# Five ordered places, a later set of splits, and four more convolution taps off VectorE in a two-layer trunk

## The chip, the cores and the metric

The kernel runs on one core of a Trainium2 chip. The core has five engines that run their own instruction lists and meet through semaphores: TensorE (PE in the profile; its weight loads are listed apart, as PEld), VectorE (DVE), ScalarE (ACT), GpSimd (POOL) and SyncE (SP), which here issues nearly all transfers. Matmuls write to PSUM, a memory of few 128x512 banks; the other operands lie in SBUF. The metric is the time of one execution on the device in microseconds, the median of several executions.

## What is computed

The input x has 1024 tokens of 1024 channels in float32. Layer 0 feeds one projection to two branches, layer 1 is a convolution module:

```python
# layer 0
u, gate_s, q, k, v, gate_r = split(rmsnorm(x) @ w_ab)
y  = gelu(s5(u))                                  # diagonal complex state space, chunks of 64 tokens
ys = y * sigmoid(y @ glu_w + glu_b) * silu(gate_s)
yr = headnorm(retention(rope(q), rope(k), v)) * silu(gate_r)
x1 = x + concat(ys, yr) @ w_out
# layer 1
a, b, g = split(rmsnorm(x1) @ w_c)
c  = causal_depthwise_conv(a * sigmoid(b), width=31) + bias
z  = silu(layernorm_channels(c)) * silu(g)
x2 = x1 + z @ w_out_c
out = rmsnorm(x2)
```

The matmuls keep float32 accuracy: each operand is split into a high part rounded to the matmul's format (h) and the rest (l), and each product is three matmuls, wh x xh, wh x xl and wl x xh (L224 to L226).

## The kernel before, in words

Channels lie on the 128 partitions, in eight blocks of 128; tokens run along the free dimension in two halves of 512, so nearly every tile is 128x512. Names carry the block and the half: `cv6_1` is block 6 of half 1. The trace leaves these numbers out; the lists of instructions shown below keep a half or block and a running number of the tile.

A weight block is loaded by SP as `wf` (128x1024), rounded on ACT to `wh`, and `wl = wf - wh` is made on POOL, for some matrices on DVE (L214). Weights that both halves use are stored as `lo` and loaded again in half 1 (L181, L199). Buffers of one tag go round in a ring: a load waits on SP until the last reader of the buffer it takes is done, and what SP has behind it waits too. The tag `tp` has three buffers. It serves, one after the other, the loads `yr0f`, the first five taps of each convolution block, and the gate loads `gl` of blocks 0 to 2 of half 1.

The program is written stage by stage, and a scheduler orders each engine's list by the position in the program, by priorities (`self.at`) and by a model of durations. `self.order` adds pairs: on that engine's list, the first instruction (name of the output and how manyth write of it) comes after the second. A pair sets an order on one engine only. `issue_after` does the same for one instruction or a group of them.

The places that are touched:

- *The end of the state space and retention* (350 to 530 us). POOL makes the rotary product `qswp` (L1153) and the rest `wl` of the weights for v (L214). DVE makes `yn`, the input of the gelu (L1039 to L1042), and `kraw` (L1138), a projection taken from PSUM. SP stores blocks of gated sums (`t_d`, L1049) and loads `gs`, from which sums of gating weights are made, and `yp`, the next part of y; the gelu of `yp` (L1031) stands on ACT ahead of copies of v from PSUM (L1188), for whose bank PE waits (L1185).
- *The gated unit* (530 to 620 us), in `layer0_back_and_layer1`. PE forms block products `mm_glu`. DVE combines them with earlier sums into `mm_gluy` (half 0, L1453) and `mm_gluz` (half 1, L1470), which takes a product from its PSUM bank and so lets PE use the bank again. `gated` (L1396) then passes each through a tanh on ACT, a product with the gate `yg` made on POOL (L1401), and two instructions on DVE (L1414, L1418). `load_split` (L1346) loads the eight retention blocks `yr0f` and splits them: `yr0h` on ACT, `yr0l` on DVE (L1334). The output projection `mm_wo` multiplies `ys`, then `yr`.
- *The convolution* (640 to 1066 us). `conv` (L1566) does two blocks at a time. ACT makes taps 0 to 4, POOL adds them, and ACT copies the sum into a PSUM accumulator `cv`. DVE adds the other 26 taps, one `scalar_tensor_tensor` each (L1607): shifted u times the tap's weight, plus `cv`. From block 4 on, the `pilot`, a mean over the first four blocks, is taken off ahead of the last tap (L1596), which writes `co`. Block 7 of half 1 is the last; its last tap is in `conv_norm_wide` and goes into the channel sum `cs` as well (L1687 to L1689). `cq` is the sum of squares (L1693). PE sums both over the channels (`cst`, L557), and from them come the mean and the scale of the normalisation. Ahead of these two sums PE has matmuls of the last projection's half 0 (`mm_oc`), and behind them 66 more. The additions `x` (L1769) take `mm_oc` from PSUM and add `x1l`, loaded by SP.

Of the kernel before, what the change touches and what calls it, by code (L numbers as in the profile page):

```python
# [11 lines left out]
F32 = mybir.dt.float32  # L12
# [3 lines left out]
ALU = mybir.AluOpType  # L16
# [3 lines left out]
P = 128  # L20
# [13 lines left out]
LO_V = {f"g{i}" for i in range(1, 10)} | {"u4", "u5", "u6", "wos", "wor"}  # L34
NORM_TAP = 23, 11
G0 = 3


LANES = 2


def s5_order():
# [28 lines left out]
def un(ap):  # L71

    return ap.rearrange("p (c a) -> p a c", a=LANES)


def nat(ap):

    return ap.rearrange("p (a c) -> p a c", a=LANES)

# [15 lines left out]
class Trunk:  # L95
# [148 lines left out]
    def run(self):  # L244
        tc, nc, A = self.tc, self.nc, self.A
        self.ps_mm = self.pool("ps_mm", 3, PSUM)
        self.cp = self.pool("cp")
        self.wp = self.pool("wp")
        self.opA = self.pool("opA", 16)
        self.dram = self.pool("dram", 1, DRAM)  # L250

        self.ident = self.cp.tile([P, P], F32, name="ident")
        make_identity(nc, self.ident)
        self.ones = self.cp.tile([P, P], F32, name="ones")
        nc.vector.memset(self.ones[:], 1.0)
        self.ones_r = self.cp.tile([P, P], F32R, name="ones_r")
        nc.vector.tensor_copy(self.ones_r[:], self.ones[:])
        self.epst = self.cp.tile([P, 1], F32, name="epst")
        nc.vector.memset(self.epst[:], EPS)
        self.mhalf = self.cp.tile([P, KB], F32, name="mhalf")  # L260
        nc.vector.memset(self.mhalf[:], -0.5)
        self.warm = self.cp.tile([P, 1], F32, name="warm")
        nc.scalar.copy(self.warm[:], self.ones[:, 0:1])

        dt = lambda n, shape: self.dram.tile(shape, F32, name=n)
        self.u_d = dt("u_d", [8, 8, 16, 8, P])
        self.y_d = dt("y_d", [8, 8, 16, 8, P])
        self.k_d = dt("k_d", [8, 112 + P, P])
        self.gs_d = dt("gs_d", [D, T])
        self.gr_d = dt("gr_d", [D, T])  # L270
        self.yn_d = dt("yn_d", [D, T])
        self.yr_d = dt("yr_d", [D, T])
        self.t_d = dt("t_d", [2, 2, HALF, T])
        self.x1_d = dt("x1_d", [D, T])

        with ExitStack() as mid:
            self.mid = self.pool("mid", 1, stack=mid)
            with ExitStack() as st:
                self.layer0_front(st)
            with ExitStack() as st:  # L280
                self.ps_aux = self.pool("ps_aux", 5, PSUM, stack=st)
                self.retention(st)
        with ExitStack() as st:
            self.layer0_back_and_layer1(st)
        self.order(s5_order())

    def order(self, pairs):

# [1047 lines left out]
    def layer0_back_and_layer1(self, st):  # L1336
# [54 lines left out]
        def spare(name, n):  # L1391
            return ps_cv.tile([P, HALF], F32, name=name, tag=("cv", "cn")[n % 2])

        held = []

        def gated(nb, h, z, turned=False):  # L1396
            yg = lp.tile([P, HALF], F32, name=f"yg{nb}_{h}", tag="u", bufs=5)
# [63 lines left out]
        for m in range(2):  # L1461
            pss = [self.bank(f"mm_glu5{2 * m + a}", aux=False) for a in range(2)]
            for i, x in ((5, t1), (3, b22)):
                w = wn()
                for a in range(2):
                    n = 2 * m + a
                    product(pss[a], w, a, x, i == 3)
                    if i == 5:
                        z = spare(f"mm_gluz{n}", n)
                        v.tensor_tensor(nat(z[:]), un(u3[n][:]), un(pss[a][:]), op=ALU.add)  # L1470
                        gated(4 + n, 1, z, True)
                    else:
                        v.tensor_tensor(pss[a][:], u2[n][:], pss[a][:], op=ALU.add)
                        glu_end = gated(n, 1, pss[a])
        yr = [load_split([self.yr_d[rows(k), hs(h)] for k in range(KB)], f"yr{h}", h, False) for h in range(2)]


        hx = [None, None]
# [87 lines left out]
        def conv(h, n2):  # L1566
# [4 lines left out]
            for nb in (n2, n2 + 1):  # L1571
# [14 lines left out]
                        nc.scalar.copy(acc[:], s0[:])  # L1586
                accs_.append(acc)
                outs.append(opB.tile([P, HALF], F32, name=f"co{nb}_{h}", tag="B0"))
            for k in range(NT[h], CONV_K):
                for i, nb in enumerate((n2, n2 + 1)):  # L1590
                    dst = outs[i] if k == CONV_K - 1 else accs_[i]
                    tap = us[i][:, k:k + HALF], cw[:, nb, k:k + 1]
                    if k == CONV_K - 1 and late:
                        v.tensor_tensor(accs_[i][:], accs_[i][:], s0s[i][:], op=ALU.add)
                    if k == CONV_K - 1 and n2 >= 4:
                        v.tensor_tensor(accs_[i][:], accs_[i][:], pilot[h][:], op=ALU.subtract)  # L1596

                    if (h, nb, k) == (1, KB - 1, CONV_K - 1):
                        self.last_tap = *tap, accs_[i], dst
                        continue  # L1600

                    ahead = (h, n2) == (0, 6) and k >= NORM_TAP[i]
                    if k == NT[h] and late:
                        v.tensor_scalar(dst[:], *tap, None, op0=ALU.mult)
                        continue
                    with self.tc.issue_after(self.norm_first.ins) if ahead else nullcontext():
                        v.scalar_tensor_tensor(dst[:], *tap, accs_[i][:], op0=ALU.mult, op1=ALU.add)  # L1607
# [392 lines left out]
```

## Time and profile before

| | us |
|---|---|
| median of 3 runs (1140.91 to 1143.72) | 1142.86 |
| the profiled execution | 1140.13 |
| its span in the trace | 1138.3 |
| PE busy | 1119.0 |
| DVE busy | 832.9 |
| POOL busy | 640.0 |
| ACT busy | 492.3 |
| mean granted clock of PE | 0.997 |

The profile is of one execution. "Busy" counts the time in which an engine works at an instruction; an instruction's line is that of the kernel's text, often of a helper. In a timeline a row gives the start, the duration, engine, line, operation, output and inputs, the count of equal instructions run together, and in brackets the idle time before and what ended it. Overlapping starts show that an instruction's time has a part that the next one hides: a tap of 748 ns starts every 0.66 us.

### The profile page before, as it was taken

Reading aid. Unit: us, or ns where it says so; the run is one execution under the profiler, and the core shown is the slowest. Engines: PE = TensorE matmul, PEld = TensorE weight load, DVE = VectorE, ACT = ScalarE, POOL = GpSimd, SP = SyncE. Lnnn points to the kernel's source line nnn. Section 1 sums busy time; section 2 is a strip of 40 time slices with the busy share of each in tenths; the row PEclk is TensorE's granted clock in tenths of the full one; section 3 lists DMA queues with packets and bytes.
Section 4 is the critical chain, followed back from the end, with each engine's and each line's share of the span. In section 5 each row is a group of like instructions: output and inputs, shape, how many; then the busy total and the mean of one; then the engine's idle time right before and its main releaser. Section 6 shows DMA issues by size and latency. Waiting matters only on the chain.

```text
span 1138.3 us, 17193 instructions
## 1 busy us (share of the span) xinstructions
PE 1119.0 (98%) x6278; PEld 979.4 (86%) x6278; DVE 832.9 (73%) x1478; ACT 492.3 (43%) x723; POOL 640.0 (56%) x448
## 2 busy tenths in 40 slices
PE   9999999999999999999999999999999999999897
PEld 7888888888888889898888888888888888888786
DVE  7973967777417469587669523599999899999744
ACT  6422433333223231333546324455536676444673
POOL 2059999888136454332674110688534568677663
PEclk9999999999999999999999999999999999999999
DMA  9345555553487866869998987666678655367865
GB/s 356 111 132 158 195 181 180 170 176 133 150 263 251 302 221 176 314 194 348 390 354 290 339 298 268 222 218 211 221 269 293 222 188 173 111 205 243 285 225 189
DMA packets 118181, 262.51 MB, mean 231 GB/s; under 512 B 10704, under 2 KB 42320, under 8 KB 117456
## 3 DMA queue, kind: packets, MB, share of 16 engines
q1 hardware_dynamic: 114640, 248.82, 64.8%
q10 hardware_dynamic: 3456, 12.58, 2.7%
q8 instruction: 49, 0.80, 0.3%
q14 instruction: 36, 0.29, 0.1%
HBM read 182.53 MB, written 74.65 MB: 226 GB/s over the span
## 4 chain that ended last, share of the span: by engine, by line
PE 74%; DMA 10%; DVE 8%; ACT 3%; issue 2%; POOL 1%; SPq 1%; POOLq 0%; DVEq 0%; ACTq 0%
PE mm_g L224 6%; PE mm_g L225 6%; PE mm_g L226 6%; PE mm_wo L225 5%; PE mm_wo L224 5%; PE mm_wo L226 5%; DMA yp<-y_d 2%; PE mm_b L225 2%; PE mm_b L226 2%; PE mm_a L226 2%; PE mm_a L225 2%; PE mm_b L224 2%; PE mm_a L224 2%; PE mm_oc L226 2%; PE mm_oc L225 2%
## 5 line engine op out<-in xcount | busy, mean ns | idle before, releaser
L1607 DVE SCALAR_TENSOR_TENSOR cv<-u,convw,cv 128x512 f32<-128x512 f32 x398 | 273.0, 748 | 6.5 <-ACT cv L1586 4.5
L1580 POOL TENSOR_TENSOR tp<-tp,tp 128x512 f32<-128x512 f32 x64 | 83.1, 1298 | 33.8 <-ACT tp L1579 32.8
L224 PE MATMUL mm_g<-xh,wh_g 128*128 128x512 f32 x256 | 97.9, 382 | 0.0
L225 PE MATMUL mm_g<-xl,wh_g 128*128 128x512 f32 x256 | 97.0, 379 | 0.0
L226 PE MATMUL mm_g<-xh,wl_g 128*128 128x512 f32 x256 | 95.7, 379 | 0.0
L485 POOL TENSOR_TENSOR s1q<-s1q,s1q 128x512 f32<-128x512 f32 x12 | 17.6, 1470 | 79.4 <-ACT s1q L480 79.4
L1579 ACT ACTIVATE tp<-u,convw 128x512 f32<-128x512 f32 x64 | 45.4, 718 | 34.5 <-POOL tp L1580 33.8
L224 PEld LDWEIGHTS mm_g<-xh,wh_g 128*128 128x128 f32 x256 | 48.8, 191 | 6.8 <-issue 0.2
L435 DVE TENSOR_TENSOR gt<-mm_g,R 128x512 f32<-128x512 f32 x32 | 21.9, 687 | 44.5 <-PE mm_g L226 44.4
L226 PEld LDWEIGHTS mm_g<-xh,wl_g 128*128 128x128 f32 x256 | 48.4, 189 | 6.9
L225 PEld LDWEIGHTS mm_g<-xl,wh_g 128*128 128x128 f32 x256 | 48.4, 189 | 6.6
L226 PE MATMUL mm_oc<-zh,wl_woc 128*128 128x512 f32 (+1 forms) x144 | 51.0, 357 | 0.3 <-DMA wl_woc<-lo_woc 0.3
L214 POOL TENSOR_TENSOR wl_glu<-wf_glu,wh_glu 128x1024 fp32r<-128x1024 f32 x14 | 33.9, 2423 | 30.9 <-ACT wh_glu L213 30.9
L225 PE MATMUL mm_oc<-zl,wh_woc 128*128 128x512 f32 (+1 forms) x144 | 51.1, 356 | 0.0
L224 PE MATMUL mm_oc<-zh,wh_woc 128*128 128x512 f32 (+1 forms) x144 | 51.0, 366 | 0.0
L224 PE MATMUL mm_g<-h1h,wh_cg 128*128 128x512 f32 x128 | 48.9, 382 | 0.0
L224 PE MATMUL mm_wo<-ysh,wh_wos 128*128 128x512 f32 x128 | 48.9, 382 | 0.0
L225 PE MATMUL mm_b<-h1l,wh_cb 128*128 128x512 f32 x128 | 48.7, 381 | 0.2
L225 PE MATMUL mm_u<-xl,wh_u 128*128 128x512 f32 x128 | 48.1, 380 | 0.7 <-DVE xl L358 0.7
L226 PE MATMUL mm_b<-h1h,wl_cb 128*128 128x512 f32 x128 | 48.6, 380 | 0.0
L225 PE MATMUL mm_wo<-ysl,wh_wos 128*128 128x512 f32 x128 | 48.5, 379 | 0.0
L226 PE MATMUL mm_wo<-ysh,wl_wos 128*128 128x512 f32 x128 | 48.5, 379 | 0.0
(528 smaller groups left out, 3590.0 us busy)
## 6 DMA issues: line engine op xcount, KB each, us to landing
wf_g<-w_ab SPq DMA_DIRECT2D x16, 512.0 KB, 6.0
wf_wos<-w_out SPq DMA_DIRECT2D x16, 512.0 KB, 4.2
wf_wor<-w_out SPq DMA_DIRECT2D x16, 512.0 KB, 5.3
wf_cb<-w_c SPq DMA_DIRECT2D x16, 512.0 KB, 4.1
wf_ca<-w_c SPq DMA_DIRECT2D x16, 512.0 KB, 5.2
wf_woc<-w_out_c SPq DMA_DIRECT2D x16, 512.0 KB, 7.2
wf_v<-w_v SPq DMA_DIRECT2D x12, 512.0 KB
wf_cg<-w_c SPq DMA_DIRECT2D x11, 512.0 KB, 4.2
```

The lines of the kernel that those rows point to most:

```text
L214: self.low_made = lo[i].tensor_tensor(wl[:].rearrange(fl)[:, c], wf[:, c], h.bitcast(F32), op=ALU.subtract)
L224: nc.tensor.matmul(ps, wh[:, kb, :], xh, start=start, stop=False, **more)
L225: nc.tensor.matmul(ps, wh[:, kb, :], xl, start=False, stop=False, **more)
L226: self.last_mm = nc.tensor.matmul(ps, wl[:, kb, :], xh, start=False, stop=stop, **more)
L435: nc.vector.tensor_tensor(nat(gt[:, c]), un(ps[:]), nat(self.R[:, c]), op=ALU.mult)
L485: nc.gpsimd.tensor_tensor(a, a, sq[:], op=ALU.add)
L1579: nc.scalar.mul(sk[:], u[:, k:k + HALF], cw[:, nb, k:k + 1])
L1580: gp.tensor_tensor(s0[:], s0[:], sk[:], op=ALU.add)
L1607: v.scalar_tensor_tensor(dst[:], *tap, accs_[i][:], op0=ALU.mult, op1=ALU.add)
```

## The change

`MORE = {(1, 6): 4}` gives four further taps, 5 to 8, of blocks 6 and 7 of half 1 to ACT, which multiplies them into `te` tiles of the ring `tp`, and POOL, which adds them and takes the pilot off. DVE has eight taps fewer there and adds `te` where it took the pilot off. `ORDER` adds four pairs to the order. The splits of `yr0` are issued behind the third `mm_gluz` sum, `zs_[2]`. (The title's five places are the four pairs and this one.)

```diff
@@ -34,9 +34,16 @@
 LO_V = {f"g{i}" for i in range(1, 10)} | {"u4", "u5", "u6", "wos", "wor"}
 NORM_TAP = 23, 11
 G0 = 3
+MORE = {(1, 6): 4}
 
 
 LANES = 2
+ORDER = (
+    ('DVE', ('kraw_3', 0), ('yn_2', 0)),
+    ('SP', ('gs1_3', 0), ('t_d', 7)),
+    ('DVE', ('cv6_0', 23), ('h1l0_1', 0)),
+    ('Pool', ('qswp_0', 0), ('wl_v0_0_1', 0)),
+)
 
 
 def s5_order():
@@ -282,7 +289,7 @@
                 self.retention(st)
         with ExitStack() as st:
             self.layer0_back_and_layer1(st)
-        self.order(s5_order())
+        self.order(s5_order() + list(ORDER))
 
     def order(self, pairs):
 
@@ -1391,7 +1398,7 @@
         def spare(name, n):
             return ps_cv.tile([P, HALF], F32, name=name, tag=("cv", "cn")[n % 2])
 
-        held = []
+        held, zs_ = [], {}
 
         def gated(nb, h, z, turned=False):
             yg = lp.tile([P, HALF], F32, name=f"yg{nb}_{h}", tag="u", bufs=5)
@@ -1467,12 +1474,12 @@
                     product(pss[a], w, a, x, i == 3)
                     if i == 5:
                         z = spare(f"mm_gluz{n}", n)
-                        v.tensor_tensor(nat(z[:]), un(u3[n][:]), un(pss[a][:]), op=ALU.add)
+                        zs_[n] = v.tensor_tensor(nat(z[:]), un(u3[n][:]), un(pss[a][:]), op=ALU.add)
                         gated(4 + n, 1, z, True)
                     else:
                         v.tensor_tensor(pss[a][:], u2[n][:], pss[a][:], op=ALU.add)
                         glu_end = gated(n, 1, pss[a])
-        yr = [load_split([self.yr_d[rows(k), hs(h)] for k in range(KB)], f"yr{h}", h, False) for h in range(2)]
+        yr = [load_split([self.yr_d[rows(k), hs(h)] for k in range(KB)], f"yr{h}", h, False, zs_[2] if h == 0 else None) for h in range(2)]
 
 
         hx = [None, None]
@@ -1586,14 +1593,26 @@
                         nc.scalar.copy(acc[:], s0[:])
                 accs_.append(acc)
                 outs.append(opB.tile([P, HALF], F32, name=f"co{nb}_{h}", tag="B0"))
-            for k in range(NT[h], CONV_K):
+            more, others = MORE.get((h, n2), 0), []
+            for nb, u in zip((n2, n2 + 1), us) if more else ():
+                with self.at(105000 + 100000 * h + 100 * nb + 50):
+                    e0 = lp.tile([P, HALF], F32, name=f"te{nb}_{h}_0", tag="tp", bufs=3)
+                    nc.scalar.mul(e0[:], u[:, NT[h]:NT[h] + HALF], cw[:, nb, NT[h]:NT[h] + 1])
+                    for k in range(NT[h] + 1, NT[h] + more):
+                        ek = lp.tile([P, HALF], F32, name=f"te{nb}_{h}_{k}", tag="tp", bufs=3)
+                        nc.scalar.mul(ek[:], u[:, k:k + HALF], cw[:, nb, k:k + 1])
+                        gp.tensor_tensor(e0[:], e0[:], ek[:], op=ALU.add)
+                    gp.tensor_tensor(e0[:], e0[:], pilot[h][:], op=ALU.subtract)
+                others.append(e0)
+            for k in range(NT[h] + more, CONV_K):
                 for i, nb in enumerate((n2, n2 + 1)):
                     dst = outs[i] if k == CONV_K - 1 else accs_[i]
                     tap = us[i][:, k:k + HALF], cw[:, nb, k:k + 1]
                     if k == CONV_K - 1 and late:
                         v.tensor_tensor(accs_[i][:], accs_[i][:], s0s[i][:], op=ALU.add)
                     if k == CONV_K - 1 and n2 >= 4:
-                        v.tensor_tensor(accs_[i][:], accs_[i][:], pilot[h][:], op=ALU.subtract)
+                        v.tensor_tensor(accs_[i][:], accs_[i][:], (others[i] if more else pilot[h])[:],
+                                        op=ALU.add if more else ALU.subtract)
 
                     if (h, nb, k) == (1, KB - 1, CONV_K - 1):
                         self.last_tap = *tap, accs_[i], dst
```

Where the change moves instructions, the lists show it. DVE in the gated unit, from `mm_gluy_6005` (block 6 of half 0) to the first gluz sum, `mm_gluz_6064`, for which PE waits at 600 us; before:

```order
L1334 TENSOR_TENSOR yr0l_6279<-yr0f_6276,yr0h_6278 128x512
L1414 TENSOR_SCALAR mm_gluy_6005<-mm_gluy_6005,yg_0_6007 128x512
L1334 TENSOR_TENSOR yr0l_6285<-yr0f_6282,yr0h_6284 128x512
L1453 TENSOR_TENSOR mm_gluy_6031<-gu_3_5527,mm_glu_6018 128x512
L1334 TENSOR_TENSOR yr0l_6291<-yr0f_6288,yr0h_6290 128x512
L1418 TENSOR_SCALAR ysl_0_6015<-mm_gluy_6005,ysh_0_6014 128x512
L1414 TENSOR_SCALAR mm_gluy_6031<-mm_gluy_6031,yg_0_6033 128x512
L1470 TENSOR_TENSOR mm_gluz_6064<-gu_0_5524,mm_glu_6044 128x512
L1334 TENSOR_TENSOR yr0l_6297<-yr0f_6294,yr0h_6296 128x512
```

and after the change:

```order
L1421 TENSOR_SCALAR mm_gluy_6005<-mm_gluy_6005,yg_0_6007 128x512
L1460 TENSOR_TENSOR mm_gluy_6031<-gu_3_5527,mm_glu_6018 128x512
L1425 TENSOR_SCALAR ysl_0_6015<-mm_gluy_6005,ysh_0_6014 128x512
L1421 TENSOR_SCALAR mm_gluy_6031<-mm_gluy_6031,yg_0_6033 128x512
L1477 TENSOR_TENSOR mm_gluz_6064<-gu_0_5524,mm_glu_6044 128x512
```

The first three `yr0l` splits left the stretch ahead of the sum, and the fourth no longer follows it; all eight stand behind `mm_gluz_6180`, the third sum.

DVE at the end of the convolution, from the addition `x` of output block 2 to the two sums that PE waits for (`cv_1_10260` and `cv_1_10277` are the accumulators of blocks 6 and 7); before:

```order
L1769 TENSOR_TENSOR x_2_0_9882<-mm_oc_0_0_9884,x1l_0_9880 128x512
L1607 TENSOR_SCALAR cv_1_10277<-u_1_8863,convw,cv_1_10277 128x512
L1607 TENSOR_SCALAR cv_1_10260<-u_1_8796,convw,cv_1_10260 128x512
L1607 TENSOR_SCALAR cv_1_10277<-u_1_8863,convw,cv_1_10277 128x512
L1596 TENSOR_TENSOR cv_1_10260<-cv_1_10260,pilot_10133 128x512
L1607 TENSOR_SCALAR cv_1_10277<-u_1_8863,convw,cv_1_10277 128x512
L1607 TENSOR_SCALAR co_1_10262<-u_1_8796,convw,cv_1_10260 128x512
L1607 TENSOR_SCALAR cv_1_10277<-u_1_8863,convw,cv_1_10277 128x512 x6
L1596 TENSOR_TENSOR cv_1_10277<-cv_1_10277,pilot_10133 128x512
L1687 TENSOR_TENSOR cvs_bank<-cv_1_10277,cs_1_10238 128x512
L1688 TENSOR_SCALAR co_1_10279<-u_1_8863,convw,cv_1_10277 128x512
L1689 TENSOR_SCALAR cs_1_10238<-u_1_8863,convw,cvs_bank 128x512
```

and after the change:

```order
L1788 TENSOR_TENSOR x_2_0_9882<-mm_oc_0_0_9884,x1l_0_9880 128x512
L1626 TENSOR_SCALAR cv_1_10277<-u_1_8863,convw,cv_1_10277 128x512 x5
L1614 TENSOR_TENSOR cv_1_10277<-cv_1_10277,te_1_0_10292 128x512
L1706 TENSOR_TENSOR cvs_bank<-cv_1_10277,cs_1_10238 128x512
L1707 TENSOR_SCALAR co_1_10279<-u_1_8863,convw,cv_1_10277 128x512
L1708 TENSOR_SCALAR cs_1_10238<-u_1_8863,convw,cvs_bank 128x512
L1712 TENSOR_TENSOR cq_10223<-cq_10223,cvq_bank 128x512
L1788 TENSOR_TENSOR x_3_0_9923<-mm_oc_0_0_9925,x1l_0_9921 128x512
```

Nine instructions instead of sixteen stand from behind that addition up to `cs`, and the next addition `x` moved behind `cq`.

POOL in the same stretch, between the second `wl_woc` and the fifth (`wl_woc_0_9874`), with the sums of block 7's further taps in `te_1_0_10292`; before:

```order
L1638 TENSOR_TENSOR cq_10223<-cq_10223,cvq_1_10227 128x512
L1638 TENSOR_TENSOR cq_10223<-cq_10223,cvq_1_10231 128x512
L1638 TENSOR_TENSOR cq_10223<-cq_10223,cvq_1_10235 128x512
L214 TENSOR_TENSOR wl_woc_0_9793<-wf_woc_0_9791,wh_woc_0_9792 128x1024
L1650 TENSOR_TENSOR cq_10223<-cq_10223,cvq_1_10239 128x512
L1650 TENSOR_TENSOR cq_10223<-cq_10223,cvq_1_10243 128x512
L214 TENSOR_TENSOR wl_woc_0_9833<-wf_woc_0_9831,wh_woc_0_9832 128x1024
L214 TENSOR_TENSOR wl_woc_0_9874<-wf_woc_0_9872,wh_woc_0_9873 128x1024
```

and after the change:

```order
L1604 TENSOR_TENSOR te_1_0_10292<-te_1_0_10292,te_1_6_10294 128x512
L1657 TENSOR_TENSOR cq_10223<-cq_10223,cvq_1_10227 128x512
L1604 TENSOR_TENSOR te_1_0_10292<-te_1_0_10292,te_1_7_10297 128x512
L1657 TENSOR_TENSOR cq_10223<-cq_10223,cvq_1_10231 128x512
L221 TENSOR_TENSOR wl_woc_0_9793<-wf_woc_0_9791,wh_woc_0_9792 128x1024
L1604 TENSOR_TENSOR te_1_0_10292<-te_1_0_10292,te_1_8_10300 128x512
L1657 TENSOR_TENSOR cq_10223<-cq_10223,cvq_1_10235 128x512
L221 TENSOR_TENSOR wl_woc_0_9833<-wf_woc_0_9831,wh_woc_0_9832 128x1024
L1605 TENSOR_TENSOR te_1_0_10292<-te_1_0_10292,pilot_10133 128x512
L1669 TENSOR_TENSOR cq_10223<-cq_10223,cvq_1_10239 128x512
L221 TENSOR_TENSOR wl_woc_0_9874<-wf_woc_0_9872,wh_woc_0_9873 128x1024
```

Four instructions on `te_1_0_10292` came in between; the four on `te_1_0_10280` stand ahead of the second `wl_woc`.

## The prediction

> **What bounds the kernel now.** I read the page first, then the list of waits of TensorE, then each listed wait in the timeline of the engine it waits for. The page says which engine to watch:
>
> ```profile
> span 1138.3 us, 17193 instructions
> PE 1119.0 (98%) x6278; PEld 979.4 (86%) x6278; DVE 832.9 (73%) x1478; ACT 492.3 (43%) x723; POOL 640.0 (56%) x448
> L1607 DVE SCALAR_TENSOR_TENSOR cv<-u,convw,cv 128x512 f32<-128x512 f32 x398 | 273.0, 748 | 6.5 <-ACT cv L1586 4.5
> L1580 POOL TENSOR_TENSOR tp<-tp,tp 128x512 f32<-128x512 f32 x64 | 83.1, 1298 | 33.8 <-ACT tp L1579 32.8
> L1579 ACT ACTIVATE tp<-u,convw 128x512 f32<-128x512 f32 x64 | 45.4, 718 | 34.5 <-POOL tp L1580 33.8
> ```
>
> TensorE (PE) works 1119.0 of 1138.3 us, so only the 19 us in which it stands still, or runs slowly, can be won without taking matmuls away, and this change takes none away. The list of its waits (line, what it waited for, total us, times, longest) says where they lie:
>
> ```profile
> PE cst L557 <- DVE cs L1689: 3.2, 1, 3.2
> PE mm_glu L224 <- DVE mm_gluz L1470: 2.3, 1, 2.3
> PE mm_v L1185 <- ACT v L1188: 1.3, 2, 1.0
> ...
> PE mm_v L1210 <- POOL wl_v L214: 0.7, 1, 0.7
> ...
> PE mm_glu L224 <- ACT v L1188: 0.4, 1, 0.4
> ```
>
> These are single waits, each at one place, and each part of the change stands near one of them. The largest costs more than its 3.2 us, as the timeline of PE shows (start, us, line, operation, count):
>
> ```profile
> 1062.57 0.38 PE L226 MATMUL mm_oc<-zh,wl_woc 128*128 128x512 f32 x1
> 1066.16 2.03 PE L557 MATMUL cst<-cs,ones 128*128 128x512 f32 x2 [3.22 <-DVE cs L1689]
> 1067.98 1.86 PE L557 MATMUL cst<-cq,ones 128*128 128x512 f32 x2
> 1068.91 1.15 PE L224 MATMUL mm_oc<-zh,wh_woc 128*128 128x512 f32 x1
> 1069.89 0.38 PE L225 MATMUL mm_oc<-zl,wh_woc 128*128 128x512 f32 x1
> ...
> 1099.82 0.38 PE L226 MATMUL mm_oc<-zh,wl_woc 128*128 128x512 f32 x1
> 1100.04 1.02 PE L557 MATMUL rf_R<-s2q,ones 128*128 128x512 f32 x2
> ...
> 1101.11 0.38 PE L225 MATMUL mm_oc<-zl,wh_woc 128*128 128x512 f32 x1
> ```
>
> The last rows price the column sum where nobody waits: from 1100.04 one sum and one matmul of 512 columns take 1.07, and such a matmul 0.22 (1099.82 to 1100.04), so the sum takes 0.85. Without a wait, the two sums would start at 1062.57 + 0.22 = 1062.79 and the L225 matmul behind them at 1062.79 + 2 x 0.85 + 0.22 = 1064.71. It starts at 1069.89. The place costs 5.18 us: 3.4 idle and 1.8 slow. The windows show the slow part (PE busy, weight loads, DVE, ACT, POOL, then the granted clock, DMA share, GB/s):
>
> ```profile
> 600.00:601.00 1.00, 0.91 (x4) 0.83 (x5) 1.00 (x2) 1.00 (x3) 1.00 (x1) 1.00 0.98 352
> 1067.00:1068.00 1.00, 1.00 (x3) 0.30 (x2) 0.90 (x2) 0.58 (x2) 0.88 (x1) 0.50 1.11 383
> 1069.00:1070.00 1.00, 1.00 (x4) 0.47 (x3) 0.04 (x1) 0.92 (x2) 1.00 (x2) 0.68 1.00 352
> ```
>
> Behind the idle 3.4 us the clock is 0.50 until about 1069.6, while behind the 2.3 us at 600 it is 1.00. The Trainium skill ("TensorE: Matmul & The Clock Gate", Part 1: The HAM clock gate) has it that the clock falls to half after an idle window of about 3.4 us, which runs freely, and comes back after about as long a busy one; this trace agrees with 0.50 and 1.00. Because the window runs freely, by that page some executions of the kernel before need not have fallen to half, and there the place would be worth 3.4, not 5.2; no run here shows it, and the sum below keeps 5.2.
>
> **The change part by part.** *Taps on ScalarE and GpSimd.* DVE is what PE waits for at 1066.16, and it is busy without a gap for 59.6 of the 60 us ahead:
>
> ```profile
> 1000.00:1060.00 60.00, 60.00 (x280) 52.52 (x279) 59.56 (x91) 27.41 (x40) 43.27 (x31) 1.00 0.72 244
> ...
> 1030.56 13.35 DVE L1607 SCALAR_TENSOR_TENSOR cv<-u,convw,cv 128x512 f32<-128x512 f32 x20
> ...
> 1054.06 0.69 DVE L1769 TENSOR_TENSOR x<-mm_oc,x1l 128x512 f32<-128x512 f32 x1 [0.41 <-DMA x1l<-x_d]
> ...
> 1065.36 0.74 DVE L1689 SCALAR_TENSOR_TENSOR cs<-u,convw,cvs_bank 128x512 f32<-128x512 f32 x1
> ...
> 1066.62 0.68 DVE L1693 TENSOR_TENSOR cq<-cq,cvq_bank 128x512 f32<-128x512 f32 x1
> ```
>
> Twenty taps in 13.35 us make 0.667 each. Eight fewer take 5.3 us from DVE, and the pilot's subtraction becomes an addition of the same shape. So cs ends at 1066.10 - 5.3 = 1060.8, and cq, which no x addition precedes any more, at 1061.5: 2.0 and 2.1 us before PE wants them (1062.79 and 1063.64). A second way agrees: the x addition of 1054.06 now has nine instructions behind it up to cs instead of sixteen, 1054.67 + 9 x 0.667 = 1060.7. The whole 5.2 is then won; the bounds are 0 and 5.2.
>
> That holds if POOL delivers. ACT gets eight taps, 8 x 0.72 = 5.8 us, in a stage where it works 27.4 of 60. POOL gets eight additions and subtractions, 8 x 1.3 = 10.4 us, and has 60 - 43.3 = 16.7 free. They stand between work PE needs, so I went through POOL's new list from 1022 on with these durations:
>
> ```profile
> 1035.59 0.38 PE L224 MATMUL mm_oc<-zh,wh_woc 128*128 128x512 f32 x1
> ...
> 1047.11 2.37 POOL L214 TENSOR_TENSOR wl_woc<-wf_woc,wh_woc 128x1024 fp32r<-128x1024 f32 x1 [1.18 <-ACT wh_woc L213]
> ...
> 1046.78 1.00 SPq L1757 DMA_DIRECT2D x1l<-x_d  x1
> ```
>
> The sums of te7 end near 1049.6 (DVE wants them near 1058); the wl_woc of 1047.11 ends near 1053.2 instead of 1049.5, and PE first uses it as the 89th matmul after 1035.59, at 1035.59 + 88 x 0.2157 = 1054.6; the next ends near 1060.7 against 1061.9; POOL's own part of cs near 1057, against the 1058.8 at which DVE adds to it. The spare time shrinks to 1.2 to 1.8 us, but stays. The x1l load of 1046.78 now has a gl load ahead on SP that wants a buffer of the tp ring; the last POOL addition that frees it ends near 1044.7, so the load isn't later. The gl loads behind it wait for the two te tiles until about 1058, and the wf_woc loads behind those follow 2 to 4 us later; their weights serve matmuls after 1074. Behind the sums the 66 matmuls and the normalisation chain stand as before. I charge nothing.
>
> *The yr0 splits behind the third gluz sum.* DVE, ahead of 600, and what follows:
>
> ```profile
> 594.33 0.68 DVE L1334 TENSOR_TENSOR yr0l<-yr0f,yr0h 128x512 fp32r<-128x512 f32 x1
> ...
> 596.86 1.37 DVE L1334 TENSOR_TENSOR yr0l<-yr0f,yr0h 128x512 fp32r<-128x512 f32 x1
> ...
> 599.35 0.68 DVE L1470 TENSOR_TENSOR mm_gluz<-gu,mm_glu 128x512 f32<-128x512 f32 x1
> 599.95 2.29 DVE L1334 TENSOR_TENSOR yr0l<-yr0f,yr0h 128x512 fp32r<-128x512 f32 x1
> ...
> 601.65 1.73 POOL L1401 TENSOR_TENSOR yg<-yg,yn 128x512 f32<-128x512 f32 x1
> ...
> 610.55 0.38 PE L226 MATMUL mm_glu<-y22h,wl_glu 128*128 128x512 f32 x1
> ...
> 622.66 1.22 DVE L214 TENSOR_TENSOR wl_wos<-wf_wos,wh_wos 128x1024 fp32r<-128x1024 f32 x1
> ```
>
> Three splits leave the stretch ahead of gluz: starts at 594.33, 595.52 (0.60 each) and 596.86 (1.29 to the next start), 2.5 us, of which 0.4 to 0.6 may come back as waits for ACT's sigmoids. Gluz then ends near 598.0 instead of 600.03: 1.9 won, between 1.3 and 2.3. What it puts at risk: a yg addition moves ahead of the last wl_glu on POOL (2.37, as the wl_woc above). Its load, issued at 599.8, lands by my estimate at 603.3 to 605.1, so wl_glu ends at 607.0 to 608.8, and PE wants it at 610.55 - 1.9 = 608.65: up to 0.2. The splits that went behind delay nothing on PE's list, which takes the last two among matmuls of the next block; the wl_wos of 622.66 is in time by 0.4. I charge 0.4 for both, between 0 and 1.5.
>
> *kraw behind yn on DVE.* One row each changes place:
>
> ```profile
> 482.75 1.64 DVE L1041 TENSOR_TENSOR yn<-yn,yn 128x512 f32<-128x512 f32 x1
> ...
> 464.06 1.28 ACT L1031 ACT_TABLE_LOAD   x1 [4.84 <-DMA yp<-y_d]
> ...
> 882.34 0.19 PEld L225 LDWEIGHTS mm_b<-h1l,wh_cb 128*128 128x128 f32 x1 [0.43 <-DVE h1l L1514]
> ```
>
> The y chain, whose step at 482.75 is slow (1.64), goes 0.6 earlier, kraw 0.6 later, and nothing waits for kraw on PE. It can only help at the two waits behind the gelu on ACT, 0.3 (of the 1.3) and 0.4: 0 to 0.7, taken 0.3. *gs behind the eighth t_d store on SP.* The yp load stands behind both before and after, so the ACT step at 464.06, which held the v copy for the 1.0 us wait, gains at most what t_d gains: 0 to 1.0, taken 0.3. *A tap behind h1l on DVE.* h1l 0.66 earlier removes the late weight load at 882.34: 0.2 to 0.4, taken 0.2. *qswp behind wl_v on POOL.* POOL's list is the same row for row there, since qswp already stood behind that half; the 0.7 wait for the later wl_v stays. 0.
>
> Sum: 5.2 + 1.9 - 0.4 + 0.3 + 0.3 + 0.2 = 7.5. Between 610 and 1062 the list has PE waiting at 882 alone, so what is won at 600 goes through to the end unless a load there is late. The profiled execution took 1140.13 (span 1138.3), 2.7 below the median of the three runs, 1142.86. 1140.13 - 7.5 = 1132.6, and at the median 1135.4.
>
> **The rivals.** *A: POOL takes DVE's place at the end of the convolution.* If each added POOL instruction costs 0.4 more (as one of the same shape took 1.73 at 601.65), POOL is 3 us later: PE then waits 1.6 at the fifth wl_woc and about as long at the next, and 5.2 shrinks to 2. Total gain 4.3 or less: 1138.5 to 1141. For it: spare times of 1.2 to 1.8; against: 16.7 free.
>
> *B: the wait at 600 moves to wl_glu.* If the yg load lands 2 us later than I take it, in a stretch with a DMA share of 0.98, 1.9 is given back: 1137.3.
>
> *C, slower: POOL holds up the convolution taps on DVE.* The split of 599.95 took 2.29 instead of 0.68 beside POOL's work. If each of the eight new POOL instructions held a tap for that difference, 8 x 1.6 = 12.9 us, DVE would lose what it gains and more; it turns slower than before from 5.3 + 2.3 = 7.6 us on, and 12.9 would give 1142.9 + 5.3 = 1148. Against it: the twenty taps at 1030.56 ran at 0.667 while POOL was busy nearly throughout. The Trainium skill ("SBUF — State Buffer", Who interferes with whom) says that a DVE instruction with two SBUF inputs contends with a GpSimd instruction that reads SBUF, and one with a single SBUF input does not. A tap adds to an accumulator in PSUM, the split reads two SBUF tiles, so by that rule C would not happen, and the trace agrees with 0.667 and 2.29.
>
> *D: nothing happens at 1066, since cs waits for something else.* The x1l load (0.41 waited at 1054.06) could land 5 us later behind the gl load: 1140.6.
>
> **How the numbers follow.** Chances: forecast 0.65, A 0.13, B 0.10, C 0.05, D 0.07. A measurement here tells 0.3%, 3.4 us, from no change: faster means below 1139.4, slower above 1146.3. Forecast, B and half of A are faster (0.81), half of A and D the same (0.13), C and an unforeseen mishap slower (0.06). The low end takes all upper bounds, 5.2 + 2.3 + 0.7 + 1.0 + 0.4 = 9.6, to 1133.2, and a run spread of 1; the high end reaches to A.
>
> **What would show it.** Right: at the cst sums PE's wait is gone and the windows keep clock 1.00; the gluz wait falls below 0.5; the 0.7 at wl_v is unchanged. Wrong: PE waiting for wl_woc or cs from POOL between 1050 and 1063, for wl_glu near 607, DVE taps above 0.7, or a long wait of DVE for x1l.

## The result, and the profile after

| | us |
|---|---|
| before, median of 6 runs (1140.53 to 1145.45) | 1143.29 |
| after, median of 6 runs (1132.11 to 1138.03) | 1134.74 |
| ratio of the runs, with its 95% interval | 0.9933 [0.9910, 0.9956] |
| the profiled execution after | 1138.03 |

The kernel became faster by 0.67%, and the forecast of 1135.4 is 0.7 us off. The profiled execution is the slowest of its six, while that of before, 1140.13, lies below all six of its kernel. So the two spans differ by 2.1 us and the medians by 8.5. A difference between two single profiles has to be read place by place. Up to the first gate matmul of half 1 the execution after is 2.5 us behind that of before (867.54 against 865.03). Of this, 1.5 arise between PE's first matmul for v and its first `mm_glu`, a stage that takes from 188.6 to 192.8 us in the fourteen profiles of this document and, in the mean, as long with the pairs for `kraw` and `gs` (190.2) as without (190.4). The page and the list of TensorE's waits after the change:

```profile
span 1136.2 us, 17205 instructions
PE 1117.1 (98%) x6278; PEld 978.9 (86%) x6278; DVE 828.1 (73%) x1470; ACT 498.0 (44%) x731; POOL 647.3 (57%) x456
```

```profile
PE mm_glu L231 <- ACT sg L1416: 1.6, 1, 1.6
PE mm_v L1217 <- POOL wl_v L221: 1.5, 2, 1.2
PE mm_oc L233 <- DMA wl_woc<-lo_woc: 1.2, 1, 1.2
PE mm_v L1192 <- ACT v L1195: 1.1, 1, 1.1
...
PE mm_glu L231 <- ACT v L1195: 0.9, 1, 0.9
PE mm_wo L231 <- ACT yr0h L1339: 0.9, 1, 0.9
PE mm_glu L231 <- DVE mm_gluz L1477: 0.7, 1, 0.7
```

The largest wait of before, 3.2 for `cs`, is gone, and the one for `mm_gluz` fell from 2.3 to 0.7. The one for a reload of `wl_woc` grew from 0.3 to 1.2, that for `wl_v` from 0.7 to 1.5, and 0.9 for `yr0h` and 1.6 for `sg` are new. The last stands at 555 us, ahead of the places that the later splits touch; kernels without the splits have it too (1.4 with the taps alone, 1.3 with the pairs alone). The timeline of PE at the end of the convolution, from the first matmul of the last projection's half 0 to the first sum of the final normalisation, and the windows there:

```profile
1037.73 0.38 PE L231 MATMUL mm_oc<-zh,wh_woc 128*128 128x512 f32 x1
...
1064.71 0.38 PE L233 MATMUL mm_oc<-zh,wl_woc 128*128 128x512 f32 x1
1064.92 1.02 PE L564 MATMUL cst<-cs,ones 128*128 128x512 f32 x2
1065.78 1.02 PE L564 MATMUL cst<-cq,ones 128*128 128x512 f32 x2
...
1085.31 0.48 PE L233 MATMUL mm_oc<-zh,wl_woc 128*128 128x512 f32 x1 [1.24 <-DMA wl_woc<-lo_woc]
...
1097.93 1.02 PE L564 MATMUL rf_R<-s2q,ones 128*128 128x512 f32 x2
```

```profile
1000.00:1060.00 60.00, 60.00 (x280) 52.52 (x279) 59.61 (x91) 33.63 (x49) 51.00 (x37) 1.00 0.71 235
...
1066.00:1068.00 2.00, 2.00 (x9) 1.39 (x8) 0.70 (x1) 1.70 (x4) 2.00 (x1) 1.00 1.04 399
```

Nobody waits at the sums, and the clock stays at 1.00. This stretch of PE, from the first `mm_oc` to `rf_R`, takes 1097.93 - 1037.73 = 60.20 us; before it took 1100.04 - 1035.59 = 64.45. So 4.25 us are won here between these two executions, of the 5.2 forecast: 3.4 ahead of the first sum (30.57 against 27.19) and 0.9 behind it (33.88 against 33.01).

### The profile page after: what moved, and what is told of

The parts are those of the page before. It is cut to its first block, busy times and chain, and to the rows that moved or that the text cites. A ratio compares the mean times of both kernels' runs of the same rounds, so it can differ in the third digit from the quotient of the medians.

```text
span 1136.2 us, 17205 instructions
## 1 busy us (share of the span) xinstructions
PE 1117.1 (98%) x6278; PEld 978.9 (86%) x6278; DVE 828.1 (73%) x1470; ACT 498.0 (44%) x731; POOL 647.3 (57%) x456
## 4 chain that ended last, share of the span: by engine, by line
PE 73%; DMA 13%; DVE 7%; ACT 3%; issue 2%; POOL 1%; SPq 1%; POOLq 0%; DVEq 0%; ACTq 0%
PE mm_g L231 7%; PE mm_g L232 7%; PE mm_g L233 7%; PE mm_wo L231 5%; PE mm_wo L233 5%; PE mm_wo L232 5%; PE mm_a L233 2%; DMA yp<-y_d 2%; PE mm_b L232 2%; PE mm_a L231 2%; PE mm_b L233 2%; PE mm_a L232 2%; PE mm_b L231 2%; PE mm_oc L233 2%; PE mm_oc L231 2%; PE mm_oc L232 2%
## 5 line engine op out<-in xcount | busy, mean ns | idle before, releaser
L1626 DVE SCALAR_TENSOR_TENSOR cv<-u,convw,cv 128x512 f32<-128x512 f32 x390 | 267.7, 749 | 5.4 <-ACT cv L1593 3.4
L233 PE MATMUL mm_a<-h1h,wl_ca 128*128 128x512 f32 x128 | 48.6, 380 | 0.3 <-DMA wl_ca<-lo_ca 0.3
```

The costliest lines, as they stand in the source:

```text
L233: self.last_mm = nc.tensor.matmul(ps, wl[:, kb, :], xh, start=False, stop=stop, **more)
```

## The experiments

All kernels here compute the whole reference. Ratios are to the kernel before, with 95% intervals; a gain in us is (1 - ratio) x 1143. Single executions of one kernel scatter by about 2 us (1132.1 to 1138.0 for the changed one), so one part's gain is known to some 1.5 to 3 us.

| kernel | ratio | gain, us |
|---|---|---|
| the whole change | 0.9933 [0.9910, 0.9956] | 7.7 |
| further taps alone | 0.9987 [0.9972, 1.0003] | 1.5 |
| later yr0 splits alone | 0.9987 [0.9971, 1.0003] | 1.5 |
| the four pairs alone | 0.9966 [0.9953, 0.9978] | 3.9 |
| two further taps instead of four, alone | 0.9974 [0.9955, 0.9992] | 3.0 |
| the pairs for kraw and gs alone | 0.9989 [0.9975, 1.0003] | 1.3 |
| the pair of the tap and h1l alone | 0.9971 [0.9955, 0.9987] | 3.3 |
| taps, and an x addition moved back | 0.9960 [0.9936, 0.9985] | 4.6 |
| whole, and that addition moved back | 0.9919 [0.9902, 0.9936] | 9.3 |
| the same less the pair of the tap and h1l | 0.9960 [0.9944, 0.9975] | 4.6 |
| whole less the taps | 0.9946 [0.9931, 0.9961] | 6.2 |
| whole, qswp moved further | 0.9929 [0.9913, 0.9944] | 8.1 |

**The parts alone.** The theory of the prediction: the taps bring 5.2, the splits 1.5, the pairs 0.8. The first three kernels each keep one part:

```diff
 # taps only
-ORDER = ( ... four pairs ... )
+ORDER = ()
-... load_split(..., zs_[2] if h == 0 else None)
+... load_split(..., None)
```

> The four further taps of blocks 6 and 7 alone, without the four ordered pairs and with the yr0 splits where they were. Theory (the place at the sums cst costs 3.4 us idle and 1.8 us at half clock, and POOL keeps up): PE's wait for cs is gone, the granted clock stays 1.00 there, and the median is 5.2 us below the kernel before (4.5 to 5.5). Rival, idle time alone: 3.4 us below. Rival, POOL takes DVE's place: PE waits for wl_woc or cs from POOL between 1050 and 1063, and 2 us or less are won.

> The yr0 splits behind the third gluz sum alone. Theory: the wait of 2.3 us for gluz shrinks to 0.1 to 0.7, up to 0.9 us comes back as waits for a late yr0h or wl_glu behind it, and the median is 1.0 to 1.9 us below before. Rival, given back later: waits of about 2 us arise between 605 and 630, and the median is within 0.5 us of before.

> The four ordered pairs alone. Theory: 0.8 us below before (0 to 2.0), since each pair can win no more than one wait of 0.2 to 1.0 us, and the pair of qswp changes no list. Rival, the pairs do harm in the profiled execution after (waits for v on ACT of 1.1 and 0.9 us instead of 1.3 and 0.4): 0 to 1 us above before.

The gains were 1.5, 1.5 and 3.9. Their sum, 6.9, is near the whole's 7.7, but the shares are not those forecast: the taps bring less than a third of their 5.2, the pairs five times their 0.8. Two questions follow: where the taps' gain went, and what in the pairs brings so much.

**Where the taps' gain went.** In the taps-only kernel no wait at the sums is left either. The timeline of PE behind them, then DVE's (with its wait) and SP's rows of the load that DVE waits for:

```profile
1079.39 0.95 PE L226 MATMUL mm_oc<-zh,wh_woc 128*128 128x512 f32 x2 [0.70 <-ACT zh L1334]
```

```profile
1073.74 0.69 DVE L1783 TENSOR_TENSOR x<-mm_oc,x1l 128x512 f32<-128x512 f32 x1 [5.40 <-DMA x1l<-x_d]
```

```profile
1065.72 1.26 SPq L1771 DMA_DIRECT2D x1l<-x_d  x2
```

An addition `x` of the output stands on DVE inside the normalisation chain. Its `x1l`, issued at 1065.72, arrives 8.0 us later (two loads are issued there together, the second within 1.3 us); DVE stands still for 5.40 with the rest of the chain behind it, and PE waits for the `zh` at the chain's end, 0.70 here and 0.50 at 1082.38. Two theories: DVE was relieved too much, so that fewer taps do as well; or the held addition is at fault. Two further taps tell the first, and moving that addition behind the chain's product (`zz`) the second:

```diff
-MORE = {(1, 6): 4}
+MORE = {(1, 6): 2}
```

> Two further taps of blocks 6 and 7 instead of four, without pairs and with the yr0 splits where they were. DVE has four taps fewer, so cs comes 2.65 us earlier, and PE's wait at cst should be 0.6 to 0.9 us. Theory with the clock: an idle time this short leaves the granted clock at 1.00, so 2.65 + 1.8 = 4.4 us are won. Rival, idle time alone: 2.65 us.

```diff
 # taps only, with one pair
+ORDER = (('DVE', ('x2_5_0', 0), ('zz1_1', 1)),)
```

> The four further taps alone, as in the run that had them alone, and one more pair: the addition x of output block 5 on DVE comes behind the second subtraction of the normalisation of half 1, so that the chain from cst to the first zl doesn't stand behind the x1l load. Theory (the taps' gain was given back because DVE waited 5.4 us for x1l inside that chain): no wait for zh between 1079 and 1086, and 3.5 to 5 us below before, against 1.5 to 2.6 of the taps alone. Rival, the chain is late through ACT's own order: the same time as the taps alone.

With two taps the list has no wait of PE at the sums: they start at 1067.24, 0.50 behind the matmul of 1066.74, where 0.22 is the matmul itself, so 0.28 are left of the 3.2.

```profile
1066.74 0.38 PE L228 MATMUL mm_oc<-zh,wl_woc 128*128 128x512 f32 x1
1067.24 1.13 PE L559 MATMUL cst<-cs,ones 128*128 128x512 f32 x2
```

It gained 3.0, with an interval that overlaps that of four taps. Its stretch from the first `mm_oc` to `rf_R` takes 59.96, no longer than with four taps (60.20), so the profile doesn't show that four are needed. With the addition moved back, the waits for `zh` are gone and 4.6 is gained instead of 1.5. The intervals overlap here as well; the profiles agree with the held addition as the cause, in that kernel: the stretch takes 63.32 with the taps alone and 60.56 with the addition moved back. In the whole change, whose lists the planner set anew, it costs little: `x1l` was issued 1.45 us behind the start of the sums, against 3.15 in the taps-only kernel, and DVE waits 0.28:

```profile
1071.41 0.69 DVE L1788 TENSOR_TENSOR x<-mm_oc,x1l 128x512 f32<-128x512 f32 x1 [0.28 <-DMA x1l<-x_d]
```

```profile
1066.37 1.25 SPq L1776 DMA_DIRECT2D x1l<-x_d  x2
```

So the pair was added to the whole change, and the taps were taken out of it:

```diff
 # whole, and the addition moved back
 ORDER = (
     ...
+    ('DVE', ('x2_5_0', 0), ('zz1_1', 1)),
```

> The whole change and the same additional pair for the addition x of output block 5. Theory: 0.5 to 1.5 us below the whole change (0.9933 of before, so 0.992 to 0.993), because executions whose x1l load lands late no longer lose by it. Rival, no late x1l in most executions: the same as the whole change.

```diff
 # whole less the taps
-MORE = {(1, 6): 4}
+MORE = {}
```

> The four pairs and the later yr0 splits, without the further taps. If the parts add up: 3.5 + 1.3 = 4.8 below before, some 1138 (ratio 0.9958), PE waits 2.5 to 3.2 us for cs and in some executions the clock is 0.5 behind it. If the taps are worth the full 5.2 of the prediction in company, it is 5 us above the whole change, 1140 (ratio 0.998).

The first is at 1134.60, against 1134.74 for the change itself: no difference that these runs can tell. Without the taps the time is 1136.38. In company, then, the taps are worth 7.7 - 6.2 = 1.5, as they were alone, or 3.1 with the addition moved back, each difference known to some 3 us only. PE's timeline without the taps:

```profile
1034.09 0.38 PE L231 MATMUL mm_oc<-zh,wh_woc 128*128 128x512 f32 x1
...
1064.44 1.12 PE L564 MATMUL cst<-cs,ones 128*128 128x512 f32 x2 [2.99 <-DVE cs L1708]
1065.40 1.02 PE L564 MATMUL cst<-cq,ones 128*128 128x512 f32 x2
...
1096.04 1.02 PE L564 MATMUL rf_R<-s2q,ones 128*128 128x512 f32 x2
```

The stretch takes 61.95 in this execution, only 1.75 more than with the taps. Two things make the difference to the 5.2. First, PE waited 2.99, and the clock did not fall: the two starts at the sums are 0.96 apart. Second, no wait for `wl_woc` follows, while with the taps PE waits 1.24 at 1085.31. The reload is issued when PE has read the old contents of its buffer, so it comes earlier too, but it meets other transfers. The windows ahead of it, of the changed kernel and of the one without taps (the last two columns are DMA share and GB/s):

```profile
1076.00:1078.00 2.00, 2.00 (x11) 1.76 (x10) 1.34 (x3) 2.00 (x4) 2.00 (x2) 1.00 1.03 414
1078.00:1080.00 2.00, 2.00 (x11) 1.75 (x10) 1.93 (x4) 2.00 (x4) 1.37 (x3) 1.00 1.05 418
```

```profile
1076.00:1078.00 2.00, 2.00 (x11) 1.76 (x10) 2.00 (x4) 2.00 (x4) 2.00 (x3) 1.00 0.84 258
1078.00:1080.00 2.00, 2.00 (x11) 1.76 (x10) 2.00 (x4) 1.97 (x4) 2.00 (x3) 1.00 0.67 227
```

With the taps the transfers of this place are packed into 414 and 418 GB/s, without them 258 and 227. SP's list shows what packs them. A load `gl` of the changed kernel waits there 3.0 us for the buffer of a `te` tile, until DVE has added the tile (1058.73 + 0.70). The first of the weight loads `wf_woc` behind it then waits 2.5 for POOL and is issued 2.5 us ahead of PE's first sum; without the taps it is issued 11.3 us ahead of it. The two loads with the taps, and the second without:

```profile
1059.45 0.32 SPq L1757 DMA_DIRECT2D gl<-gs_d  x1
...
1062.40 0.33 SPq L196 DMA_DIRECT2D wf_woc<-w_out_c  x1
```

```profile
1053.19 0.33 SPq L196 DMA_DIRECT2D wf_woc<-w_out_c  x1
```

That the traffic is what makes the reload late is read from these rows; no run isolates it, and with two taps SP waits 6.4 for such tiles while PE waits 0.6 for a reload. In every kernel with four taps PE waits for reloads: 1.2 (the change), 1.6 and 1.3 (addition moved back, alone and in the whole), 1.4 (qswp moved further), 1.9 (without the h1l pair), 0.3 (taps only, where PE had lost its time before); in the seven profiles without further taps it is 0.3 at most.

All profiles together price the place better than any two. Ahead of the first sum the stretch takes 30.1 to 30.6 without further taps and 27.2 with four, so 2.9 to 3.4 is won. Behind the first sum it takes 33.2 to 34.5 in the five profiles in which the clock fell, 31.6 and 32.4 in the two in which it didn't, and 33.0 to 34.0 with four taps (36.1 with the taps alone). Most of what the slow clock had cost is so given back to later waits. The whole stretch is 63.7 in the mean of the seven profiles without further taps, and 60.6 in the mean of the five with four in which no addition is held: 3.1.

**What in the pairs brings 3.9.** The theory after those runs: the pair of the tap and `h1l`, which changes far more rows than its one; the rival: `kraw` and `gs`, which stand at the two waits behind the gelu.

```diff
 ORDER = (
-    ('DVE', ('kraw_3', 0), ('yn_2', 0)),
-    ('SP', ('gs1_3', 0), ('t_d', 7)),
     ('DVE', ('cv6_0', 23), ('h1l0_1', 0)),
-    ('Pool', ('qswp_0', 0), ('wl_v0_0_1', 0)),
 )
```

> Only the pairs of kraw behind yn (DVE) and of gs behind the t_d store (SP), nothing else of the change: three rows move on each of these two lists, and no other list changes. As the prediction had it: 0.6 us below before (0 to 1.7). Rival, these two carry what the four pairs gave together (0.34%, 3.5 to 3.9 us): 2.5 to 4 us below, with shorter waits of PE for v between 460 and 530.

> Only the pair of the convolution tap behind h1l (DVE). As the prediction had it: 0.2 us below before (0 to 0.4), from the weight load at 882. Rival, the new order that the scheduler gives to PE, DVE and ACT around the first half's normalisation carries the gain: 2 to 4 us below, in the stretch from 715 to 1036, which took 0.9 us less in the profile of the four pairs.

The pair of the tap and `h1l` alone gained 3.3, the other two 1.3, which is not told from nothing. In company it was taken out again:

```diff
 # whole, the addition moved back, without one pair
-    ('DVE', ('cv6_0', 23), ('h1l0_1', 0)),
```

> The whole change with the further pair (x2_5_0 behind zz1_1), less the pair that puts a tap behind h1l. If that pair is worth in company what it was worth alone, this is 3.4 us above the whole with the further pair (ratio to before near 0.995, some 1138), and the interval from the first mm_g of half 1 to the first mm_oc is 0.9 us longer or, with a wait for csr at the pilot sum, some 2.5 us longer. If the 3.4 alone was mostly scatter between executions, it is 0.2 to 0.9 us above it (ratio 0.992 to 0.993).

The gain fell from 9.3 to 4.6, and the two intervals don't meet. So this pair is worth some 3.3 alone (1.5 at least) and 4.7 in company. Its wait at 882 was 0.4. The rest has another place. In the kernels with the splits alone and with the two pairs alone, PE waited 1.7 and 1.8 for `csr`, the sum of the second pilot; in the first profile of before it didn't. So before was profiled again, unchanged:

> The kernel before once more, for a second profile of it. If the wait for csr at the pilot sum (1.7 and 1.8 us in the two kernels without the h1l pair, none in the first profile of before) belongs to the list and a late gl load, a second profile of before shows one of 0 to 2 us there, with POOL waiting over 8 us for gl; if it is of those kernels alone, none, and POOL waits 6.3 again. The wait for cs is 2.7 to 3.3 either way, with or without the half clock behind it.

The second profile of before (1141.42 us) does have it: PE's list of waits, then POOL, then SP's waits and rows near 975 us.

```profile
PE cst L557 <- DVE cs L1689: 3.3, 1, 3.3
PE mm_glu L224 <- DVE mm_gluz L1470: 1.8, 1, 1.8
PE cm L1618 <- POOL csr L1616: 1.7, 1, 1.7
```

```profile
981.98 1.28 POOL L1740 TENSOR_TENSOR co<-gl,co 128x512 f32<-128x512 f32 x1 [8.45 <-DMA gl<-gs_d]
```

```profile
SPq L1738 <- DMA gs_d<-sgg: 3.6, 1, 3.6
```

```profile
974.89 0.33 SPq L1555 DMA_DIRECT2D gs_d<-sgg  x1
978.93 0.33 SPq L1738 DMA_DIRECT2D gl<-gs_d  x1
```

`sgg`, the gate of one block, is stored to `gs_d`, and `gl` loads from `gs_d`; SP holds the load until that store has landed. POOL stands 8.45 us at the product with `gl` with the tap sums and `csr` behind it, and PE waits for `csr`. In the first profile of before SP waits 1.9 for the same store:

```profile
SPq L1738 <- DMA gs_d<-sgg: 1.9, 1, 1.9
```

There POOL waited 6.34 and PE not at all. Over all eight profiles of kernels without the pair, SP's wait for this store is 3.5 to 3.6 in three, each with PE waiting 1.7 to 1.8 at the pilot sum; 2.9 in one, with PE waiting 0.2; and 1.9 to 2.0 in four, where PE doesn't wait. The Trainium skill ("DMA: Bandwidth & Descriptors", Latency and other measured facts) gives 0.2 us for an access to HBM on average and 2 us at high load, as the main part of a transfer's fixed cost. The spread here, from 1.9 to 3.6 for one and the same store, is of that size; that load on HBM makes it, no run shows.

With the pair the planner changed ACT's list where `sgg` is made. ACT there, of before and of the kernel with this pair alone (`tp_1_0_10246` is the first tap of the next block, `tp_1_4_10163` the last of the one before):

```
594 L1579 ACTIVATE tp_1_4_10163<-u_1_8729,convw 128x512
595 L1575 ACTIVATE tp_1_0_10246<-u_1_8796,vecs,convw 128x512
596 L1554 ACTIVATE sgg_0_8897<-mm_g_0_8872 128x512

594 L1583 ACTIVATE tp_1_4_10163<-u_1_8729,convw 128x512
595 L1558 ACTIVATE sgg_0_8897<-mm_g_0_8872 128x512
596 L1579 ACTIVATE tp_1_0_10246<-u_1_8796,vecs,convw 128x512
```

The tap waits for a buffer of the ring `tp` that POOL frees, and `sgg` stood behind it. Of before, and of the kernel with the pair alone:

```profile
974.47 0.81 ACT L1575 ACTIVATE tp<-u,vecs,convw 128x512 f32<-128x512 f32 x1 [2.85 <-POOL tp L1580]
975.19 0.57 ACT L1554 ACTIVATE sgg<-mm_g 128x512 f32<-128x512 f32 x1
```

```profile
970.75 0.72 ACT L1583 ACTIVATE tp<-u,convw 128x512 f32<-128x512 f32 x1 [2.85 <-POOL tp L1584]
971.38 0.58 ACT L1558 ACTIVATE sgg<-mm_g 128x512 f32<-128x512 f32 x1
972.87 0.82 ACT L1579 ACTIVATE tp<-u,vecs,convw 128x512 f32<-128x512 f32 x1 [0.91 <-POOL tp L1584]
```

Now `sgg` comes ahead of the tap, its store is issued 1.7 us earlier, counted from PE's first gate matmul of half 1, POOL waits 4.22 for `gl`, and PE waits for `csr` in none of the profiles with the pair. This explains a gain of 1.7 to 1.8 in those executions in which the store takes 3.5, of 0.2 where it takes 2.9, and of nothing elsewhere. Besides, PE needs 169.7 to 170.2 us from its first gate matmul of half 1 to the first `mm_oc` in the profiles with the pair, and 170.2 to 170.6 without it where the store is early: up to 0.9 more. Together that is 0 to 2.7 an execution, and 1.5 in the mean: 169.8 over the six profiles with the pair, 171.3 over the eight without. The gains measured, 3.3 [1.5, 5.1] and 4.7 (known to some 2.6), reach into that range with their low ends alone; what the pair brings beyond it, and where, stays open. The store's delay is read from the profiles, and the order on ACT by itself was not tried.

**qswp.** The fourth pair changes no list. Named so that it moves, in the whole change:

```diff
-    ('Pool', ('qswp_0', 0), ('wl_v0_0_1', 0)),
+    ('Pool', ('qswp_0', 0), ('wl_v0_0_3', 0)),
```

> The whole change with the further pair, and the qswp pair named so that it does move: qswp behind the wl_v of the fourth quarter. If PE's wait for wl_v near 355 is POOL's order alone, that wait (0.7 in before, up to 1.8) is gone and the time is 0.7 to 1.5 below the whole with the further pair. If qswp is wanted as early as wl_v, a wait for the rotated q or its product takes its place and the time is the same or some us longer.

The kernel that ran differs from the change in this line alone; the addition of the expectation was not moved back in it, so the change itself, 7.7, is what it compares with. In its profile the wait for `wl_v` is gone, but the time is the same (8.1 against 7.7, overlapping). The wait differs between two executions of one kernel as well, 0.7 and 0.3 in the profiles of before, and over the other kernels it goes from none with the taps alone to 2.6 in the whole less the h1l pair. A single profile without it proves nothing, and no gain is shown.

## Why the prediction was right, and which of its steps were wrong

The total was right by luck, 7.5 forecast against 7.7 [5.0, 10.3]: by the runs two errors cancelled, the taps forecast 3.7 too high and the pairs 3.1 too low. The profiles, place by place, account for less, 3.1 for the taps, 0.7 for the splits and 1.5 for the pair of the tap and `h1l`, together 5.3, near the low end of that interval. Where the rest comes from isn't shown.

*Taps, 5.2 forecast, 1.5 measured alone [-0.3, 3.2] and in company, 3.1 by the profiles.* The mechanism up to the sums was right in each point, and so was its price, 3.4 of idle time. `cs` ends at 1060.80 + 0.74 = 1061.54, 3.4 us ahead of the sums (2.0 forecast), `te` is added without a wait, and POOL has the fifth `wl_woc` ready at 1055.1 where PE needs it at 1037.73 + 88 x 0.2157 = 1056.7:

```profile
1058.73 0.70 DVE L1614 TENSOR_TENSOR cv<-cv,te 128x512 f32<-128x512 f32 x1
...
1060.80 0.74 DVE L1708 SCALAR_TENSOR_TENSOR cs<-u,convw,cvs_bank 128x512 f32<-128x512 f32 x1
```

```profile
1052.72 2.37 POOL L221 TENSOR_TENSOR wl_woc<-wf_woc,wh_woc 128x1024 fp32r<-128x1024 f32 x1
```

The step that failed is the last one, "Behind the sums the 66 matmuls and the normalisation chain stand as before. I charge nothing." Behind the sums PE now waits 1.2 for a reload of `wl_woc`, and in the taps-only kernel, for `zh`; of the 1.8 forecast there, 0.9 is won. The prediction had seen the loads that stand behind the `te` tiles on SP come later, and looked only at the matmuls that use their weights. The 5.2 was also the price of an execution in which the clock fell; where it doesn't, the place costs 3.0. The prediction named that condition and gave it no share in the sum. Rival D had the right load, `x1l` held up, at a place 20 us too early.

*Splits, 1.5 forecast, 1.5 measured [-0.3, 3.3], 0.7 by the profiles.* Gluz's wait fell from 2.3 and 1.8 in the two profiles of before to 0.72; below 0.5 was forecast. What was charged for `wl_glu` turned up at `yr0h`, which the prediction had said would delay nothing:

```profile
601.44 0.48 PE L231 MATMUL mm_glu<-y22h,wh_glu 128*128 128x512 f32 x1 [0.72 <-DVE mm_gluz L1477]
...
627.19 0.48 PE L231 MATMUL mm_wo<-yr0h,wh_wor 128*128 128x512 f32 x1 [0.88 <-ACT yr0h L1339]
```

Over the six profiles with the splits gluz's wait is 0.3 to 1.0, over the eight without it is 1.5 to 2.3, and what comes back at `yr0h` is 0 to 0.9. All that PE waits from 580 to 630 is 1.8 in the mean without the splits and 1.15 with them. So the term took its price from an execution with a long wait, and the 1.5 of the runs neither confirms nor refutes it. Rival B did happen in one kernel, the whole less the taps, with 0.7 at `wl_glu` of its 1.9.

*kraw and gs, 0.6 forecast, 1.3 measured [-0.3, 2.9].* Neither confirmed nor refuted by the runs; the stage that they stand in shows no gain in the profiles (190.2 with, 190.4 without).

*A tap behind h1l, 0.2 forecast, 3.3 measured alone and 4.7 in company.* The step priced only the wait of 0.4 beside the pair. The list of before had to be compared with the list after, engine by engine, over the 120 us behind the pair: the planner had put `sgg` ahead of a waiting tap, which accounts for up to 2.7 of the gain. In the first profile of before the wait for `csr` that this removes did not occur, so it could not be read there; POOL's 6.3 us at `gl` could.

*qswp, 0 forecast.* Its list is unchanged, as said. The prediction took a wait of 0.7 for `wl_v`, unchanged, as a sign of being right; it is 1.2 and 0.3 in the profile after.

Rival A did not occur: added POOL sums take 1.27, and PE waits for POOL nowhere between 1037 and 1065. Nor did C: the taps beside a POOL busy for 51.0 of 60 us keep their pace (seven in 4.69).

```profile
1044.89 4.69 DVE L1626 SCALAR_TENSOR_TENSOR cv<-u,convw,cv 128x512 f32<-128x512 f32 x7
```

## What to carry to other kernels

A wait that is taken away is worth what is left of it behind the next late thing. Follow the chain past the place, to the next reload that is released by the engine one makes faster and to the loads held behind a buffer that the change keeps longer, before the whole wait is booked.

A pair in a scheduler's order is not one row: compare all engines' lists behind it, and look above all for what moved past an instruction that waits.

Where parts of a change are to be priced, run each part alone and the whole without it. A right total says little about its terms, and one profile of an execution says little about waits that occur in some executions only.

## What the runs showed of the hardware

The clock didn't follow the length of the wait. PE stood 2.72 us at the sums in the kernel with the splits alone, and the clock fell to half; it stood 2.71 us at the same place with two pairs alone, and it stayed:

```profile
1069.32 1.77 PE L559 MATMUL cst<-cs,ones 128*128 128x512 f32 x2 [2.72 <-DVE cs L1703]
```

```profile
1070.00:1071.00 1.00, 1.00 (x3) 0.40 (x2) 1.00 (x2) 0.73 (x2) 0.72 (x1) 0.50 0.93 369
```

```profile
1066.97 1.13 PE L562 MATMUL cst<-cs,ones 128*128 128x512 f32 x2 [2.71 <-DVE cs L1706]
```

```profile
1067.00:1068.00 1.00, 1.00 (x2) 0.27 (x2) 1.00 (x2) 1.00 (x2) 0.06 (x1) 1.00 0.96 229
```

Of the seven profiles with a wait of 2.7 to 3.3 for `cs`, the clock fell in five and stayed in two, one of them after 2.99. It fell once after only 2.37, at the `wl_v` of the whole less the h1l pair:

```profile
356.45 0.48 PE L1217 MATMUL mm_v<-wl_v,xh 128*128 128x512 f32 x1 [2.37 <-POOL wl_v L221]
```

```profile
359.00:360.00 1.00, 1.00 (x4) 0.82 (x3) 0.96 (x2) 0.00 (x0) 1.00 (x2) 0.50 1.00 319
```

The Trainium skill ("TensorE: Matmul & The Clock Gate", Part 1: The HAM clock gate) has a window of 3.4 us that runs freely, and the clock falls after an idle one. The free run agrees with 2.72 and 2.71. That a whole window must be idle doesn't agree with the falls after 2.37 and 2.72, since neither wait can fill a window of 3.4; the measurement decides.
